# A hybrid decoder layer on one core: gate matmuls dealt one at a time, three score banks a head for one query block, and five small reorderings

## The chip, the cores and the metric

The kernel runs on one core of a Trainium2 chip. The core has a matmul engine (TensorE, PE in the rows below), a vector engine (DVE), a scalar engine (ACT), a general-purpose engine (GpSimd, POOL) and a queue engine that issues most transfers (SyncE, SP). Matmul results land in PSUM, of which the kernel uses eight banks of 128x512 float32. The metric is the device time of one execution in microseconds (us).

## The reference

One decoder layer on 1024 tokens of width 1024, all in float32:

```python
h   = rmsnorm(x, norm_mix)
(q, kc, vc, ks, vs, kw, vw, nsa_g, rq, rk, rv, rg, gate_a, gate_b) = split(h @ w_in)
A   = nsa(q, ...)        # 8 heads: compressed + selected + sliding-window attention, gated per head
B   = retention(rq, rk, rv) * silu(rg)      # 4 heads, chunks of 128, decaying state
x   = x + (sigmoid(gate_a) * (A @ w_proj_a) + sigmoid(gate_b) * (B @ w_proj_b)) @ w_out
x   = x + square(relu(rmsnorm(x, norm_mlp) @ w_up)) @ w_down
y   = rmsnorm(x, norm_final)
```

With 1024 tokens there are 16 blocks to select and 16 are selected, so the selected branch is plain causal attention. Window: 512 keys. Compressed keys: one for every 16 tokens.

## The kernel before

Every float32 matmul is made of three: an operand X is split into a rounded part (`h`, written by an ACT copy) and the rest (`l`, a DVE subtraction), and h·h, h·l and l·h are summed in one PSUM bank. The order of PE is written out by hand for the whole program; in two stretches (the first 60 us and the one called border) the other engines' order is written out too. Elsewhere a scheduler orders ACT, DVE, POOL and SP around PE's fixed order. Within an engine everything is first in, first out.

The stages, by the time of the profiled execution:

- **Start and retention (0 to 240 us).** Weights arrive in 128x1024 pieces in a ring of three buffers named `raw` (pool `wraw`) and are split into `wh` and `wl`. Token tiles are normed, transposed (`tp`) and split into `bh`, `bl`. For the first two tiles the norm factor is applied late: `ret_v` scales, `renorm_sum` (POOL, into its own buffer `yr`) and `renorm` rebuild the tile. `ret_v` makes the values `v` (ACT, then DVE) and the swish gate: `th`, a tanh on ACT, and `y` on DVE. For each chunk PE transposes queries and keys, computes `pS`, `pO` and the state `pD`, whose operand `t` is the low half of the keys (L352 on DVE).
- **Keys, values and queries (240 to 362 us).**
- **Attention and gates (362 to 760 us).** Eight query blocks, 7 down to 0, times two key groups times two pairs of heads make 32 units. A unit has `scores` (matmuls into banks named `S`, masks and a running minimum on DVE at L1008, exponentials on ACT at L1017 into `pS`, the selected, and `pW`, window and compressed, and a scaling on POOL at L1029), then, one unit later, `pv` (transposes into banks `pt` at L1064 and L1065, split by ACT at L1066 and DVE at L1067 into `ph`, `pl`, and matmuls into bank `O`). `prep_q` transposes a group's queries (L952) and splits them into `QQ` and `ql`. In between come the matmuls of the two merge gates: 32 gates of 24 matmuls of 128x512 into a bank named `gps`, each closed by a tanh on ACT (`gst`, L920). PSUM is dealt as four `S` banks, two `pt` banks, one `gps` and one `O`. From gate 15 on, odd gates use an `S` bank.
- **Projections, output and the border (760 to 960 us).** `bh`, `bl` are overwritten by the mix. In the border, eight tiles are multiplied by the second half of `w_out` (`mmu`), added to the residual (`add_x`: `x1t`, L1378), transposed two tiles later (L1342), scaled (`y`, L1346), and combined into the forms that a Strassen-like product of the next stage needs: `first_tile` for tiles 0 to 3, `second_tile` for tiles 4 to 7. `high` is the ACT copy, `lows` the DVE subtraction that follows (L1337).
- **The two MLP products (960 to 1550 us)** and the last norm.

What sets the order in the attention stage is a list of events with fractional places: each generator (`scores`, `pv`, `prep_q`, the gates) is cut at its `yield`s, `place(it, n, lo, hi)` spreads `n` pieces evenly over an interval, and PE's program is the sorted list. `GATES` says how many pieces of the gates fall in each unit's interval. A gate yields after every third matmul.

Of the kernel before, what the change touches and what calls it, by code (L numbers as in the profile page):

```python
# [9 lines left out]
F32 = mybir.dt.float32  # L10
# [7 lines left out]
P = 128  # L18
S = 1024
# [90 lines left out]
def hybrid_block(ctx: ExitStack, tc: tile.TileContext, a: dict, out: bass.AP):  # L110
# [44 lines left out]
    def mm(o, w, m, start, stop):  # L155
        T.matmul(o, w, m, start=start, stop=stop)  # L156
# [62 lines left out]
    with ExitStack() as es:  # L219
# [12 lines left out]
        with ExitStack() as e1:  # L232
# [54 lines left out]

            def renorm_sum(j, q):
                js, ks = slice(j * P, (j + 1) * P), slice(4 * q, 4 * q + 4)
                y = tpb.tile([P, 4, P], F32, name="yr", bufs=1)  # L290
                G.tensor_tensor(y, bh[:, ks, js].bitcast(F32), bl[:, ks, js].bitcast(F32), op=OP.add)
                return y

# [88 lines left out]

            def ret_v(j, c, ps):
                raw = c == 0 and j < RAW
                if raw:
                    v = tmp.tile([P, 2, 2, P], F32R, name="v", tag="v")
                    src = ps[:, :256].rearrange("p (n d) -> p n d", n=2)
                    A.activation(v[:, :, 0], src, AF.Copy, scale=rs_raw[j])
                    V.scalar_tensor_tensor(v[:, :, 1], src, rs_raw[j], v[:, :, 0], op0=OP.mult, op1=OP.subtract)
                else:  # L390
                    v = hl(ps[:, :256], "v", 2)
                th = tmp.tile([P, 256], F32, name="th", tag="th")
                A.activation(th, ps[:, 256:], AF.Tanh, scale=hrs_raw[j] if raw else 0.5)
                y = tmp.tile([P, 256], F32, name="y")
                V.scalar_tensor_tensor(y, th, 1.0, ps[:, 256:], op0=OP.add, op1=OP.mult)
                return v, y
# [44 lines left out]
            with tc.manual_schedule(engines={eng.PE, eng.Pool, eng.DVE, eng.Activation, eng.SP}):  # L441
# [20 lines left out]
                def w_hi(w):  # L462
                    A.activation(w[1], w[0], AF.Copy)
# [33 lines left out]
                lo = [split_half(y0[q], 0, q) for q in range(2)]  # L497
                warm_up(2)
                banks = [bank(j) for j in range(3)]
                w_hi(ws[1])  # L500
                w_lo(ws[0])
                ws.append(w_dma(3))
                xs.append(load_norm(3))
# [398 lines left out]
    def gate_pieces(n):  # L902
        pool = gpool["p"]
        i, th = divmod(n, 2)
        dst, ii = (ga_scr, i) if i < 8 else (gb_scr, i - 8)
        ts = slice(th * 512, (th + 1) * 512)
        gate_w(i)
        gate_w(i + 1)
        h, l = gw[i]
        if n % 2 and n >= GALT and gpool["alt"] is not None:  # L910
            ps = gpool["alt"].tile([P, 512], F32, name="gps", tag="S")
        else:
            ps = pool.tile([P, 512], F32, name="gps", bufs=1)
        parts = [(h, k, x) for k in range(KD) for x in (bh, bl)] + [(l, k, bh) for k in range(KD)]
        for m, (w, k, x) in enumerate(parts):
            mm(ps, w[:, k * P:(k + 1) * P], x[:, k, ts], m == 0, m == len(parts) - 1)
            if m % 3 == 2 and m < len(parts) - 1:
                yield
        o = gsp.tile([P, 512], F32, name="gst")
        A.activation(o, ps, AF.Tanh, scale=0.5)  # L920
        nc.sync.dma_start(dst[ii, :, th], o)
        yield
# [13 lines left out]
    with ExitStack() as e3:  # L936
# [10 lines left out]
        gpool["p"], gpool["alt"] = psO, psS  # L947

        def prep_q(qb, g):
            tp = psT.tile([P, 4, P], F32, name="pt", tag="pt")  # L950
            for h in range(4):
                T.transpose(tp[:, h], qs[qb, g][:, h], ident)  # L952
            QQ = at.tile([P, 4, P], F32R, name="QQ")
# [5 lines left out]
            if nxt < 16:  # L959
                load_q(7 - nxt // 2, nxt % 2)  # L960
            yield

        def scores(qb, g, hp, u):
            QQ, ql = qs[qb, g]
# [10 lines left out]
            for i in range(2):  # L975
# [4 lines left out]
                pS = at.tile([P, 1024], F32, name="pS", bufs=PS_S)  # L980
                pW = at.tile([P, 768], F32, name="pW", bufs=PS_S)
                G.memset(pW[:, 704:], 0.0)
                for base, KK, start, width, p in ((1, KKs, 0, cS, pS), (2, KKw, w0, cW, pW)):
                    groups = []
                    for c0 in range(0, width, 512):
                        n = min(512, width - c0)
                        groups.append([(base if c0 == 0 else base + 2, KK, start + c0, n,
                                        mask(c0, n, width, base == 2), p[:, c0:c0 + n])])
                    split = len(groups) > 1
                    if base == 2:  # L990
                        tail = (0, KKc, 0, 64, cmp_m[:, 56 - 8 * qb:120 - 8 * qb], pW[:, 640:704])
                        if groups[-1][0][3] <= 448:
                            groups[-1].append(tail)
                        else:
                            groups.append([tail])
                    exps = []
                    for gi, grp in enumerate(groups):
                        ps = psS.tile([P, 512], F32, name="S")
                        off = 0
                        done = []  # L1000
                        for b, K, c0, n, mk, o in grp:
                            done.append((b, ps[:, off:off + n], mk, o))
                            off += n
                        _, K, c0 = grp[0][:3]
                        mm(ps[:, :off], QQ[:, h], K[:, g, c0:c0 + off], True, False)
                        mm(ps[:, :off], ql[:, h], K[:, g, c0:c0 + off], False, True)
                        for b, sc, mk, o in done:
                            V.tensor_tensor_reduce(sc, sc, mk, -0.125, BIGPOS, OP.add, OP.min, mx[:, b:b + 1])  # L1008
                            exps.append((b, sc, o))
                        if gi < len(groups) - 1:  # L1010
                            yield
                    if split:
                        V.tensor_tensor(mx[:, base:base + 1], mx[:, base:base + 1], mx[:, base + 2:base + 3],
                                        op=OP.min)
                    for b, sc, o in exps:
                        m = b - 2 if b > 2 else b
                        A.activation(o, sc, AF.Exp, bias=mx[:, m:m + 1], scale=-1.0, accum_out=sums[:, b:b + 1])  # L1017
                    if base == 1:
# [66 lines left out]

        def n_scores(qb):
            sel, win = (qb + 4) // 4, (min(qb + 1, 5) + 3) // 4 + (1 if qb == 3 else 0)
            return 2 * (sel + win)

        def n_pv(qb):  # L1090
            return 2 * ((qb + 1 + min(qb + 1, 5) + 2) // 2)
# [22 lines left out]
            place(it, n_pv(qb) - 1, n, n + 1 + V_END)  # L1114
            place(it, 1, n + 1 + V_LAST, n + 1 + V_LAST)
        for n, k in enumerate(GATES):
            place(gate_it, k, n - 1, n)
        next(prep_q(7, 0))
        for ev in sorted(todo, key=lambda v: v[:2]):
            if len(ev) > 3:  # L1120
# [121 lines left out]
    with ExitStack() as e5:  # L1242
# [80 lines left out]
        with ExitStack() as e6:  # L1323
# [25 lines left out]
            def first_tile(j):  # L1349
                js = cols(j)  # L1350
                high("11", raw_t[j, 0], bh[:, :4, js], bl[:, :4, js])
                high("21", raw_t[j, 1], bh[:, 4:, js], bl[:, 4:, js])
                lows("11", "21")
                V.tensor_sub(raw_t[j, 0], raw_t[j + 4, 0], raw_t[j, 0])

# [345 lines left out]
```

## Time and profile before

| | |
|---|---|
| Median of 3 runs (lowest, highest) | 1564.6 us (1562.92, 1568.26) |
| Profiled execution, its own time | 1563.77 us |
| Profiled execution, span of its instructions | 1562.0 us |
| Mean granted PE clock | 0.999 |
| Busy share of the span: PE, DVE, ACT, POOL | 99%, 69%, 47%, 27% |
| PE matmuls | 7845 |

A row of the waits view says which engine and line waited, for whom, the total in us, how often, and the longest. A row of the timeline has the start, the duration, engine, line, operation, output<-input, shape and, in brackets, how long the engine sat idle before it and who released it. Matmuls overlap: a 128x512 matmul has a duration of 0.39 us, but in a stream of them one starts every 0.22 to 0.23 us, so PE's busy share hides waits of less than about 0.16 us and shows the rest too short.

### The profile page before, as it was taken

The numbers are of one execution on the slowest core, as the hardware profiler recorded it, in microseconds if no ns is written. First come the engines' busy times: TensorE is split into PE (matmuls) and PEld (weight loads), VectorE is DVE, ScalarE is ACT, GpSimd is POOL, SyncE is SP. The second block draws the span as 40 slices with busy tenths as digits, with TensorE's granted clock in tenths as the row PEclk, the third lists the DMA queues.
The fourth block names the chain that finished last, engine by engine and source line by source line (L and its number), as shares of the span: only waits on it lengthen the run. The fifth ranks groups of instructions, "written<-read, shape, count | busy, mean of one in ns | idle before, by whom it ended". The sixth has DMA issues, their size and how long they took to land.

```text
span 1562.0 us, 22775 instructions
## 1 busy us (share of the span) xinstructions
PE 1542.2 (99%) x7845; PEld 1293.8 (83%) x7845; DVE 1080.8 (69%) x2237; ACT 730.9 (47%) x1657; POOL 423.6 (27%) x516
## 2 busy tenths in 40 slices
PE   9999999999999999999999999999999999999997
PEld 7788888988888888888888888888888888888886
DVE  6875663765777777776765379877777667876673
ACT  6663553764677776766522234222222244443452
POOL 3120010002333333333000001744455446521320
PEclk9999999999999999999999999999999999999999
DMA  6202111342111112121644332544444597764472
GB/s 227 68 18 65 58 32 26 112 152 78 48 35 55 48 35 61 43 68 55 198 147 153 109 112 91 188 149 152 158 156 148 185 381 242 219 210 124 148 271 87
DMA packets 98900, 191.85 MB, mean 123 GB/s; under 512 B 26632, under 2 KB 30096, under 8 KB 98784
## 3 DMA queue, kind: packets, MB, share of 16 engines
q1 hardware_dynamic: 97008, 185.82, 36.2%
q0 software_dynamic: 944, 2.93, 0.5%
q10 hardware_dynamic: 832, 1.64, 0.3%
q8 instruction: 62, 1.02, 0.3%
q14 instruction: 54, 0.44, 0.1%
HBM read 140.02 MB, written 50.33 MB: 122 GB/s over the span
## 4 chain that ended last, share of the span: by engine, by line
PE 86%; DVE 6%; ACT 3%; issue 2%; POOL 0%; DMA 0%; POOLq 0%; ACTq 0%; DVEq 0%
PE mmu L156 23%; PE mm L156 20%; PE mmd L156 19%; PE gps L156 9%; PE S L156 4%; PE O L156 4%; PE pt L1065 2%; PE pt L1064 2%; ACT pW L1017 1%; PE pO L156 1%; DVE pl L1067 1%; PE pc L156 1%; DVE S L1008 1%; ACT pS L1017 0%; ACT ph L1066 0%
## 5 line engine op out<-in xcount | busy, mean ns | idle before, releaser
L1217 DVE TENSOR_TENSOR wl<-raw,wh 128x1024 fp32r<-128x1024 f32 x121 | 183.7, 1543 | 67.3 <-ACT wh L1216 66.0
L1216 ACT ACTIVATE wh<-raw 128x1024 fp32r<-128x1024 f32 x121 | 125.1, 1056 | 205.4 <-PE mmd L156 127.7
L156 PE MATMUL mmd<-wh 128*128 128x512 f32 x448 | 174.3, 389 | 0.0
L156 PE MATMUL mmd<-wl,wh 128*128 128x512 f32 x448 | 174.3, 389 | 0.0
L156 PE MATMUL mmd<-wh,wl 128*128 128x512 f32 x448 | 174.3, 389 | 0.0
L156 PE MATMUL mm<-wh,bh 128*128 128x512 f32 (+1 forms) x416 | 160.9, 390 | 1.6 <-ACT bh L271 1.0
L156 PE MATMUL mm<-wh,bl 128*128 128x512 f32 (+1 forms) x416 | 155.0, 376 | 0.0
L156 PE MATMUL mm<-wl,bh 128*128 128x512 f32 (+1 forms) x416 | 154.3, 375 | 0.0
L1067 DVE TENSOR_TENSOR pl<-pt,ph 128x512 fp32r<-128x512 f32 (+1 forms) x160 | 103.8, 649 | 35.9 <-ACT ph L1066 33.4
L1066 ACT ACTIVATE ph<-pt 128x512 fp32r<-128x512 f32 (+1 forms) x160 | 90.3, 568 | 55.2 <-PE pt L1065 54.3
L1029 POOL TENSOR_SCALAR pS<-pS,cf 128x512 f32<-128x512 f32 (+7 forms) x80 | 54.6, 688 | 225.7 <-ACT ph L1066 73.8
L1008 DVE CUSTOM_DVE_ANT_0 S<-S,edge_m 128x512 f32<-128x512 f32 (+3 forms) x192 | 100.8, 530 | 13.8 <-PE S L156 11.2
L156 PE MATMUL gps<-bl,wh 128*128 128x512 f32 x256 | 104.1, 407 | 0.0
L156 PE MATMUL gps<-bh,wh 128*128 128x512 f32 x256 | 103.1, 403 | 0.5 <-ACT gst L920 0.5
L1298 POOL TENSOR_TENSOR sf<-raw 128x512 f32<-128x512 f32 x14 | 22.9, 1633 | 294.2 <-DVE wl L1217 294.2
L156 PE MATMUL mmu<-bh,wh 128*128 128x512 f32 x256 | 99.7, 389 | 0.0
L156 PE MATMUL mmu<-bh,wl 128*128 128x512 f32 x256 | 99.6, 389 | 0.0
L156 PE MATMUL mmu<-bl,wh 128*128 128x512 f32 x256 | 99.6, 389 | 0.0
L156 PEld LDWEIGHTS mmd<-wh,wl 128*128 128x128 f32 x448 | 84.1, 188 | 17.6
L156 PEld LDWEIGHTS mmd<-wh 128*128 128x128 f32 x448 | 84.1, 188 | 17.5
L156 PEld LDWEIGHTS mmd<-wl,wh 128*128 128x128 f32 x448 | 84.1, 188 | 17.3
L156 PEld LDWEIGHTS mm<-wh,bl 128*128 128x128 f32 x416 | 78.1, 188 | 15.4 <-DVE bl L286 0.4
(362 smaller groups left out, 4033.9 us busy)
## 6 DMA issues: line engine op xcount, KB each, us to landing
raw<-u_scr SPq DMA_DIRECT2D x56, 512.0 KB, 3.9
raw<-w_down SPq DMA_DIRECT2D x41, 512.0 KB, 4.8
raw<-w_up SPq DMA_DIRECT2D x32, 512.0 KB, 3.6
u_scr<-u SPq DMA_DIRECT2D x59, 256.0 KB, 2.2
u_scr<-s SPq DMA_DIRECT2D x42, 256.0 KB, 2.0
y<-w_down SPq DMA_DIRECT2D x14, 512.0 KB, 8.3
x<-x SPq DMA_DIRECT2D x8, 512.0 KB, 5.6
qt<-q_scr SPq DMA_DIRECT2D x32, 128.0 KB, 2.4
```

Of the source, the lines that this page charges most:

```text
L156: T.matmul(o, w, m, start=start, stop=stop)
L1008: V.tensor_tensor_reduce(sc, sc, mk, -0.125, BIGPOS, OP.add, OP.min, mx[:, b:b + 1])
L1017: A.activation(o, sc, AF.Exp, bias=mx[:, m:m + 1], scale=-1.0, accum_out=sums[:, b:b + 1])
L1029: G.tensor_scalar(v, v, cf[:, b:b + 1], 1.0, op0=OP.mult, op1=OP.mult)
L1064: T.transpose(tp[:, bi * 2], p0, ident)
L1065: T.transpose(tp[:, bi * 2 + 1], p1, ident)
L1066: A.activation(ph[:, :n], tp[:, :n], AF.Copy)
L1067: V.tensor_sub(pl[:, :n], tp[:, :n], ph[:, :n])
L1216: A.activation(h[:, :n], r, AF.Copy)
L1217: V.tensor_sub(l[:, :n], r, h[:, :n])
L1298: eng.tensor_tensor(F[:, 1], x11, x21, op=OP.subtract)
```

## The change

Seven edits, in the order of the program:

1. The renormed sums (POOL) go to a `raw` buffer of the weight ring, not to `yr`. The loads of the weights `w_r1a`, which share that ring, come later in SP's order.
2. In `ret_v`, for the first two tiles, the tanh is recorded ahead of the DVE instruction that makes the low half of `v`.
3. The second piece of the first weights is copied by ACT in two halves.
4. A gate yields after every matmul; three times as many pieces are placed over the same intervals.
5. `prep_q` transposes into an `S` bank (tile `qT`), not into a `pt` bank.
6. For query block 4 a head's scores use three `S` banks and not four: selected 0 to 511; selected rest, window rest and compressed together; window 0 to 511. The instructions are the same in number and shape, but for the order.
7. In the border, the low halves of `first_tile` are made in a step of their own, `first_lows`, behind the next tile's `add_x`.

```diff
             def renorm_sum(j, q):
                 js, ks = slice(j * P, (j + 1) * P), slice(4 * q, 4 * q + 4)
-                y = tpb.tile([P, 4, P], F32, name="yr", bufs=1)
+                y = wraw.tile([P, 1024], F32, name="raw", tag="raw")[:, :512].rearrange("p (k t) -> p k t", k=4)
...
             def ret_v(j, c, ps):
                 raw = c == 0 and j < RAW
+                th = tmp.tile([P, 256], F32, name="th", tag="th")
                 if raw:
                     v = tmp.tile([P, 2, 2, P], F32R, name="v", tag="v")
                     src = ps[:, :256].rearrange("p (n d) -> p n d", n=2)
                     A.activation(v[:, :, 0], src, AF.Copy, scale=rs_raw[j])
+                    A.activation(th, ps[:, 256:], AF.Tanh, scale=hrs_raw[j])
                     V.scalar_tensor_tensor(v[:, :, 1], src, rs_raw[j], v[:, :, 0], op0=OP.mult, op1=OP.subtract)
                 else:
                     v = hl(ps[:, :256], "v", 2)
-                th = tmp.tile([P, 256], F32, name="th", tag="th")
-                A.activation(th, ps[:, 256:], AF.Tanh, scale=hrs_raw[j] if raw else 0.5)
+                    A.activation(th, ps[:, 256:], AF.Tanh, scale=0.5)
...
                 banks = [bank(j) for j in range(3)]
-                w_hi(ws[1])
+                for c in (slice(0, 512), slice(512, 1024)):
+                    A.activation(ws[1][1][:, c], ws[1][0][:, c], AF.Copy)
                 w_lo(ws[0])
...
             mm(ps, w[:, k * P:(k + 1) * P], x[:, k, ts], m == 0, m == len(parts) - 1)
-            if m % 3 == 2 and m < len(parts) - 1:
+            if m < len(parts) - 1:
                 yield
...
         def prep_q(qb, g):
-            tp = psT.tile([P, 4, P], F32, name="pt", tag="pt")
+            tp = psS.tile([P, 4, P], F32, name="qT", tag="S")
...
+        def packed(qb):
+            return qb == 4
...
+                tail = (0, KKc, 0, 64, cmp_m[:, 56 - 8 * qb:120 - 8 * qb], pW[:, 640:704])
+                if packed(qb):
+                    groups = [parts[1][:1], parts[1][1:] + parts[2][1:] + [tail], parts[2][:1]]
+                    ready = [(), (1, 0), (2,)]
+                else:
+                    groups = [[v] for v in parts[1] + parts[2]]
...
+                    for K, c0, o0, n in runs:
+                        mm(ps[:, o0:o0 + n], QQ[:, h], K[:, g, c0:c0 + n], True, False)
+                        mm(ps[:, o0:o0 + n], ql[:, h], K[:, g, c0:c0 + n], False, True)
...
         def n_scores(qb):
             sel, win = (qb + 4) // 4, (min(qb + 1, 5) + 3) // 4 + (1 if qb == 3 else 0)
-            return 2 * (sel + win)
+            return 2 * (3 if packed(qb) else sel + win)
...
         for n, k in enumerate(GATES):
-            place(gate_it, k, n - 1, n)
+            place(gate_it, 3 * k, n - 1, n)
...
                 high("11", raw_t[j, 0], bh[:, :4, js], bl[:, :4, js])
                 high("21", raw_t[j, 1], bh[:, 4:, js], bl[:, 4:, js])
+
+            def first_lows(j):
                 lows("11", "21")
                 V.tensor_sub(raw_t[j, 0], raw_t[j + 4, 0], raw_t[j, 0])
...
                     add_x(j, 1, x1t, ps)
-                    if n and n % 2 == 0:
+                    if n % 2:
+                        first_lows(j - 4)
+                    elif n:
                         lows("2", "3", "1", "4", "22")
```

Three places show how instructions move. Each list is an engine's program order, with no time in it.

**PE where one gate ends and the next begins**, in the unit of query block 7 whose heads come second (the end of gate 3; a gate's last eight matmuls read `wl`, its first reads `bh` and `wh`). Before:

```order
L156 MATMUL gps<-bh,wl 128x512 x3
L156 MATMUL O<-pl,Vw 64x256
L156 MATMUL O<-ph,Vw 128x256
L156 MATMUL O<-pl,Vw 64x256
L156 MATMUL O<-ph,Vw 128x256
L1064 MATMUL pt<-ident,pS 128x128
L1065 MATMUL pt<-ident,pS 128x128
L1064 MATMUL pt<-ident,pS 128x128
L1065 MATMUL pt<-ident,pS 128x128
L156 MATMUL O<-pl,Vw 64x256
L156 MATMUL O<-ph,Vw 128x256
L156 MATMUL O<-pl,Vc 64x256
```

One more matmul into `O` follows there, and then the next gate's first three. With the change:

```order
L156 MATMUL gps<-bh,wl 128x512 x2
L156 MATMUL O<-pl,Vw 64x256
L156 MATMUL O<-ph,Vw 128x256
L156 MATMUL O<-pl,Vw 64x256
L156 MATMUL O<-ph,Vw 128x256
L156 MATMUL gps<-bh,wh 128x512
L1075 MATMUL pt<-ident,pS 128x128
L1076 MATMUL pt<-ident,pS 128x128
L1075 MATMUL pt<-ident,pS 128x128
L1076 MATMUL pt<-ident,pS 128x128
```

Between the two gates, which write the same bank, stood four transposes and eight matmuls into `O`; now four matmuls into `O` stand there. It is so at twelve ends of gates, of query blocks 7, 6 and 5. At the end of gate 1 nothing stands between any more (before, two matmuls of 128x512 did, as in the rows at 370.93 us that the prediction shows for gate 0); gates 14 and later have other banks or a longer way.

**DVE at the end of the border**, tile 3's scaling up to tile 7's residual sum and what follows. Before:

```order
L1346 TENSOR_TENSOR y_10935<-tp,gcol 128x512
L1337 TENSOR_TENSOR bl<-y_10436,bh 128x4x128
L1337 TENSOR_TENSOR bl<-y_10935,bh 128x4x128
L1354 TENSOR_TENSOR y_10436<-y_10610,y_10436 128x512
L1378 TENSOR_TENSOR x1t<-mmu,x1t 128x512
L1217 TENSOR_TENSOR wl<-raw,wh 128x1024
```

With the change:

```order
L1357 TENSOR_TENSOR y_10928<-tp,gcol 128x512
L1391 TENSOR_TENSOR x1t<-mmu,x1t 128x512
L1348 TENSOR_TENSOR bl<-y_10429,bh 128x4x128
L1348 TENSOR_TENSOR bl<-y_10928,bh 128x4x128
L1367 TENSOR_TENSOR y_10429<-y_10603,y_10429 128x512
L1228 TENSOR_TENSOR wl<-raw,wh 128x1024
```

The sum `x1t` of tile 7 has moved ahead of the two low halves of tile 3.

**ACT at the first chunk of retention** (v, t: values and keys; `sml`: scores). Before:

```order
L388 ACTIVATE v<-mm,fac 128x2x128
L351 ACTIVATE t_831<-qk 128x2x128
L362 ACTIVATE sml<-pS 128x256
L393 ACT_TABLE_LOAD
L393 ACTIVATE th<-mm,fac 128x256
L351 ACTIVATE s<-sm 128x2x128
L351 ACTIVATE t_928<-qk 128x2x128
```

With the change:

```order
L389 ACTIVATE v<-mm,fac 128x2x128
L390 ACT_TABLE_LOAD
L390 ACTIVATE th<-mm,fac 128x256
L362 ACTIVATE sml<-pS 128x256
L351 ACTIVATE t_832<-qk 128x2x128
L351 ACTIVATE s<-sm 128x2x128
L351 ACTIVATE t_929<-qk 128x2x128
```

The table load and the tanh stand before the score copy; in the same stretch an ACT copy and a DVE subtraction of `w_r1a` (128x1024 each) have left for a place some 35 us later.

More of the change, by code (lines that the diff above doesn't have):

```diff
@@ L982, in scores @@
                 G.memset(pW[:, 704:], 0.0)
+                parts = {}
                 for base, KK, start, width, p in ((1, KKs, 0, cS, pS), (2, KKw, w0, cW, pW)):
[L984 to L993, printed above, removed]
-                        else:
[L995 to L1018, printed above, removed]
+                    parts[base] = [(base if c0 == 0 else base + 2, KK, start + c0, min(512, width - c0),
+                                    mask(c0, min(512, width - c0), width, base == 2), p[:, c0:min(width, c0 + 512)])
+                                   for c0 in range(0, width, 512)]
@@ new lines, in scores @@
+                tail = (0, KKc, 0, 64, cmp_m[:, 56 - 8 * qb:120 - 8 * qb], pW[:, 640:704])
[4 more added lines that the diff above has]
+                    groups = [[v] for v in parts[1] + parts[2]]
+                    if groups[-1][0][3] <= 448:
+                        groups[-1].append(tail)
+                    else:
+                        groups.append([tail])
+                    ready = [()] * len(groups)
+                    ready[len(parts[1]) - 1] = (1,)
+                    ready[-1] = (2, 0)
@@ new lines, in scores @@
+                exps = {0: [], 1: [], 2: []}
+                for grp, rdy in zip(groups, ready):
+                    ps = psS.tile([P, 512], F32, name="S")
+                    off, runs, done = 0, [], []
+                    for b, K, c0, n, mk, o in grp:
+                        done.append((b, ps[:, off:off + n], mk, o))
+                        if K is KKc and runs:
+                            runs[-1][3] += n
+                        else:
+                            runs.append([K, c0, off, n])
+                        off += n
+                    for K, c0, o0, n in runs:
+                        mm(ps[:, o0:o0 + n], QQ[:, h], K[:, g, c0:c0 + n], True, False)
+                        mm(ps[:, o0:o0 + n], ql[:, h], K[:, g, c0:c0 + n], False, True)
+                    for b, sc, mk, o in done:
+                        V.tensor_tensor_reduce(sc, sc, mk, -0.125, BIGPOS, OP.add, OP.min, mx[:, b:b + 1])
+                        exps[b - 2 if b > 2 else b].append((b, sc, o))
+                    for m in rdy:
+                        if len(exps[m]) > 1:
+                            V.tensor_tensor(mx[:, m:m + 1], mx[:, m:m + 1], mx[:, m + 2:m + 3], op=OP.min)
+                    for m in rdy:
+                        for b, sc, o in sorted(exps[m], key=lambda v: v[0]):
+                            A.activation(o, sc, AF.Exp, bias=mx[:, m:m + 1], scale=-1.0, accum_out=sums[:, b:b + 1])
+                    if grp is not groups[-1]:
```

## The prediction

> **What bounds the kernel now.** I read the page's first part and the windows by stage first: which engine is full, and where not. Core 0; the columns are the time, then busy us and (x) instructions of PE, its weight loads, DVE, ACT and POOL, then the PE clock, the DMA share and GB/s.
>
> ```profile
> 362.00:500.00 138.00, 135.54 (x830) 115.54 (x829) 102.90 (x357) 94.31 (x268) 44.04 (x75) 1.00 0.16 49
> 500.00:640.00 140.00, 138.44 (x878) 119.47 (x877) 107.98 (x366) 98.89 (x284) 46.76 (x91) 1.00 0.16 48
> 640.00:760.00 120.00, 117.86 (x706) 101.17 (x705) 81.76 (x294) 80.41 (x243) 37.12 (x102) 1.00 0.23 70
> 960.00:1540.00 580.00, 580.00 (x2560) 480.42 (x2559) 422.78 (x422) 191.08 (x221) 253.65 (x157) 1.00 0.56 189
> ```
>
> PE sets the time everywhere, at clock 1.00: in the last row it never stands, and the change touches nothing in that stage. In the attention stage (362 to 760 us) it stands 2.46 + 1.56 + 2.14 = 6.2 us. DVE is busy three quarters of it, so only orders and buffers can make PE wait. No edit changes how many matmuls there are; the change can move only PE's waits. So the second view is the waits of PE (total us, times, longest):
>
> ```profile
> PE pt L1065 <- POOL pS L1029: 1.7, 4, 1.0
> PE S L156 <- ACT pS L1017: 1.3, 2, 0.9
> PE O L156 <- DVE pl L1067: 0.8, 2, 0.4
> PE pD L156 <- DVE t L352: 0.8, 1, 0.8
> PE pt L952 <- DVE pl L1067: 0.7, 1, 0.7
> PE S L156 <- DVE ql L956: 0.6, 2, 0.4
> PE mm L156 <- ACT wh L463: 0.5, 1, 0.5
> PE gps L156 <- ACT gst L920: 0.5, 2, 0.2
> PE tp L1342 <- DVE x1t L1378: 0.5, 1, 0.5
> PE S L156 <- ACT QQ L955: 0.4, 1, 0.4
> ```
>
> These ten rows come to 7.8 us, half a per cent of 1562.0: all that the change aims at. What one wait costs is read from a timeline, here at the end of gate 0 (start, duration, engine, output<-input, shape; in brackets the idle time and its releaser):
>
> ```profile
> 370.25 0.85 PE L156 MATMUL gps<-bh,wl 128*128 128x512 f32 x3
> 370.93 0.39 PE L156 MATMUL S<-KKw,QQ 128*128 128x512 f32 x1
> 371.16 0.39 PE L156 MATMUL S<-KKw,ql 128*128 128x512 f32 x1
> 371.78 0.50 PE L156 MATMUL gps<-bh,wh 128*128 128x512 f32 x1 [0.23 <-ACT gst L920]
> 372.12 0.40 PE L156 MATMUL gps<-bl,wh 128*128 128x512 f32 x1
> 372.35 0.39 PE L156 MATMUL gps<-bh,wh 128*128 128x512 f32 x1
> ```
>
> and on ACT:
>
> ```profile
> 371.13 0.60 ACT L920 ACTIVATE gst<-gps 128x512 f32<-128x512 f32 x1 [0.81 <-PE gps L156]
> ```
>
> In a stream one 128x512 matmul starts 0.23 us after the other (370.93 to 371.16). After a wait the next but one starts 0.34 later (371.78 to 372.12) and then 0.23 again: a wait costs its idle time and 0.11 for refilling. The same rows give the **turn of a gate**. Its last matmul starts 0.23 before 370.93, at 370.70; the tanh starts at 371.13, 0.43 later, and takes 0.60; the next gate's first matmul starts 0.05 after it. In all 1.08 us during which PE needs other work.
>
> **The change part by part.** I sum against the profiled execution's own time, 1563.8; the median of the runs is 1564.6, so 0.8 is added at the end.
>
> *First weights in two halves.* PE waits 0.5 for this copy:
>
> ```profile
> 9.62 1.06 ACT L463 ACTIVATE wh<-raw 128x1024 fp32r<-128x1024 f32 x1 [1.02 <-DMA raw<-w_r0a]
> ```
>
> A 128x512 copy takes about 0.60 on ACT, as the tanh of that shape does, so the first half is there 0.4 earlier. **−0.4** (0 to −0.6; nothing if a later piece of the same weights is then late).
>
> *Tanh and sums.* The wait of 0.8 for `t` goes back over DVE to ACT:
>
> ```profile
> 67.14 0.41 ACT L351 ACTIVATE t<-qk 128x256 fp32r<-128x256 f32 x1
> 67.85 1.28 ACT L393 ACT_TABLE_LOAD   x1
> 69.14 0.47 ACT L393 ACTIVATE th<-mm,fac 128x256 f32<-128x256 f32 x1
> ```
>
> and on DVE:
>
> ```profile
> 69.65 0.42 DVE L395 SCALAR_TENSOR_TENSOR y<-th,mm 128x256 f32<-128x256 f32 x1 [0.77 <-ACT th L393]
> 71.33 0.75 DVE L352 TENSOR_TENSOR t<-qk,t 128x256 fp32r<-128x256 f32 x2
> ```
>
> With the change the table load stands ahead of the copy of 67.14, 0.7 earlier; DVE, which sat idle 0.77 for `th`, runs that much sooner, and the last DVE row follows in its queue. ACT's copies of `t` and the scores now come behind the load, but DVE reads them only behind `y`: the last row of DVE is 2.2 us behind the load's end (69.13). **−0.7** (0 to −0.9). A 128x1024 pair of copy and subtraction leaves this place for one some 35 us later, where nothing waits for it yet: nothing added. The Trainium skill, "ScalarE: Activation LUTs", has a figure for a table switch, but the row of 1.28 us is used.
>
> *The queries' transposes in an S bank.* The wait of 0.7 (L952, for the `pt` bank that `pl` empties) loses its cause. The rival bank is free if the heads before have been read; at a group's start they have, as `QQ` of the last group is then done with. **−0.8** with the refill (0.3 to −0.8).
>
> *Three banks a head in block 4.* The wait for the exponential `pS` is one for a bank:
>
> ```profile
> 574.78 0.40 PE L156 MATMUL S<-KKw,ql 128*128 128x512 f32 x1
> 576.06 0.36 PE L156 MATMUL S<-KKw,QQ 128*128 128x192 f32 x1 [0.89 <-ACT pS L1017]
> ```
>
> Two of these, 1.3 us, both in block 4. The bank asked for is given back by the exponential of four banks before; a head of three banks asks for one less, and the same matmuls lie between. **−1.5** (0 to −1.5).
>
> *Gates dealt one at a time, gains.* Three matmuls of a gate between pieces of a unit become one, at three times as many places, so gaps between a transpose and what DVE or POOL make of it become more even. I counted the PE work between writer and reader: it grows by about 0.46 us ahead of the `O` matmuls that wait for `pl`, and at three of the four waits for POOL's `pS`. The 0.8 (two waits) go: **−1.0**. Of the 1.7, one wait of 1.0 stays, as its distance is the same:
>
> ```profile
> 674.52 0.33 PE L1065 MATMUL pt<-ident,pS 128*128 128x128 f32 x1 [1.02 <-POOL pS L1029]
> ```
>
> The other three go: **−1.0**. Both lie between 0 and that.
>
> *The same edit, losses.* The order lists show twelve ends of gates where four matmuls into `O` now lie between the last matmul of one gate and the first of the next, which write one bank; before, four transposes and eight such matmuls did.
>
> ```profile
> 392.64 0.28 PE L156 MATMUL O<-ph,Vw 128*128 128x256 f32 x1
> 392.75 0.28 PE L156 MATMUL O<-pl,Vw 128*64 128x256 f32 x1
> ```
>
> One of these starts 0.11 to 0.12 after the other. Before: 0.23 + 12 × 0.12 = 1.6 us of cover for 1.08, no wait. Now: 0.23 + 4 × 0.12 = 0.71; PE waits 1.08 − 0.71 = 0.37, with the refill 0.48. Twelve times: **+5.8**. The least is 0, were ACT to take the tanh before its bank's last matmul, which cannot be; the least that the rows allow is 12 × 0.37 = 4.4. What stands behind the waiting matmul is all of PE's queue. While PE stands, DVE and POOL go on, so this wait also pays for a part of others, which is why I give no further loss to them.
>
> The tanh starts 0.43 after the matmul only if ACT is free. Where it has a copy to make first it is later:
>
> ```profile
> 439.32 0.85 PE L156 MATMUL gps<-bh,wl 128*128 128x512 f32 x3
> ```
>
> ```profile
> 440.32 0.60 ACT L1066 ACTIVATE ph<-pt 128x512 fp32r<-128x512 f32 x1
> 440.80 0.61 ACT L920 ACTIVATE gst<-gps 128x512 f32<-128x512 f32 x1
> ```
>
> The last of these three matmuls starts 0.39 before 440.17, at 439.78, and the tanh 1.02 after it, 0.59 too late. Four gates of the twelve stand so in the trace of before, which would be 2.4 more; but the transposes that feed `ph` now come behind the turn, so I take less than half: **+1.0** (0 to 2.4). At the end of gate 1 two 128x512 matmuls, 0.46, leave the gap, **+0.4**. The copies `QQ` and `ql` have 0.23 less PE work before their readers at two places, **+0.5** (0 to 0.5).
>
> *Border.* PE's first matmuls of the next product, tile 7's residual sum, and DVE:
>
> ```profile
> 942.55 0.39 PE L156 MATMUL mmu<-wh,bl 128*128 128x512 f32 x1
> 943.00 0.39 PE L156 MATMUL mmu<-bl,wh 128*128 128x512 f32 x1
> 944.76 0.66 PE L1342 MATMUL tp<-ident,x1t 128*128 128x128 f32 x4 [0.46 <-DVE x1t L1378]
> ```
>
> ```profile
> 942.03 1.47 DVE L1337 TENSOR_TENSOR bl<-y,bh 128x512 fp32r<-128x512 f32 x2
> 944.02 0.68 DVE L1378 TENSOR_TENSOR x1t<-mmu,x1t 128x512 f32<-128x512 f32 x1
> ```
>
> The sum `x1t` of tile 7 now stands ahead of tile 3's low halves. It needs the matmul that ends at 942.94, so it runs from about 943.0 to 943.6, and the first low half from there to 944.3. But PE's matmul of 943.00 reads that low half: it starts 1.33 later, 1.44 with the refill, while the wait of 0.46 at 944.76 and its refill of 0.16 go. **+0.8** (−0.6 if PE reads other columns of `bl` first, to +1.5).
>
> The sum: −0.4 − 0.7 − 0.8 − 1.5 − 1.0 − 1.0 = −5.4; 5.8 + 1.0 + 0.4 + 0.5 + 0.8 = +8.5; together +3.1, so 1566.9 for a profiled execution and 1564.6 + 3.1 = 1567.7 for the median. I say **1567.5**.
>
> **The rivals.** *The finer deal clears the stage.* The same pauses at the turns let DVE, ACT and POOL get ahead, and all other standing of the attention stage goes: the 6.2 us of the windows and 17 refills of 0.11, −8.1, beside −1.1 ahead of the stage, against 5.8 + 0.4 + 0.8 for the turns and the border: −2.2, 1562.4. For it: waits of 0.2 or 0.4 us are most of the rows. Against it: the longest one (674.52) keeps its distance.
>
> *The tanh stands behind copies at every turn* (the slower side). If ACT's queue has a `ph`, an exponential or a `wh` ahead of `gst`, as at 440.80, every turn is 0.59 worse: 12 × 0.59 = 7.1 in place of my 1.0, 1573.8. It decides wherever `gst` starts later than 0.43 after its last matmul. For it: ACT is two thirds busy (94.31 of 138). Against: at 371.13 it was idle 0.81 before.
>
> *The packing moves nothing.* From gate 15 on an odd gate holds one of four S banks; if that is the one missing in block 4, three banks a head wait as four did, and the queries' transposes take one more: the −1.5 fall away, 1569.2. For it: the wait is on a bank. Against it: two heads of three banks each leave more matmuls between any two uses.
>
> *The clock falls.* Twelve short pauses might throttle PE. The row at 674.52 is a pause of 1.02 us inside a window of clock 1.00, and no row shows a pause that cost clock. The Trainium skill says in "TensorE: Matmul & The Clock Gate", section "A second HAM failure mode: psum-queue depth-cycling", that a kernel which cycles through PSUM banks can idle often enough between groups for the clock to swing between half and full. By that page's window of 3.4 us, half a window's work lost at each turn would be an estimate of 12 × 1.7 = 20 us. The trace's clock of 1.00 over thirteen waits speaks against it.
>
> **How the numbers follow.** A difference of less than 0.3%, 4.7 us, can't be told from no change, so "faster" begins below 1559.9 and "slower" above 1569.3. Main forecast 0.46, its own range 1564 to 1570; clearing 0.28; tanh behind copies 0.16; packing 0.08; clock 0.02. Clearing is faster by over 0.3% only where the border's price falls away too and ACT keeps up at the turns, 0.11 of its 0.28; the main case adds 0.01: faster 0.12. Slower: 0.15 of the tanh case, 0.02 of the clock, 0.03 of the packing and 0.07 of the main case: 0.27. The rest, 0.61, is no change. The range reaches from below clearing's 1562.4 to just short of the tanh case's 1573.8: 1561 to 1573.
>
> **What would show it.** The waits of PE should have a row of `gps` for `gst` with ten or more waits and 4 to 7 us in place of 0.5; no row of L952; the row of `S` for `pS` gone or under 0.4; the row of `t` under 0.3; a wait of `mmu` for `bl` of 1 us or more near 944 in place of that of `tp`. In timelines `gst` should start 0.43 after its last matmul, where ACT is free. The prediction is wrong if the turns show no wait (the scheduler has put other work there), if `gst` comes a whole instruction later at most turns, or if the stages after 960 us change their length.

## The result: 0.56% slower, and the profile after

The changed kernel takes 1572.8 us (median of 4 runs, 1572.67 to 1573.42); the kernel before, beside it, 1563.8 (4 runs, 1562.92 to 1568.26). The ratio is 1.0056, 95% interval 1.0043 to 1.0069. It is slower by some 9 us; the forecast was 3 us slower, 1567.5 in a range of 1561 to 1573. The direction was right and the range just held, but more than half of the loss was not foreseen.

The span of the profiled execution went from 1562.0 to 1571.6 us. To see where, I cut it at PE's own instructions. These rows are the gates' matmuls, in the kernel before (the last two numbers are the first and the last start):

```profile
L156 PE MATMUL gps<-bh,wh x256: 387/395/499, 362.3 to 759.2; 128*128 128x512 f32 x128
L156 PE MATMUL gps<-bh,wl x256: 387/393/485, 368.2 to 761.2; 128*128 128x512 f32 x128
```

and in the changed kernel:

```profile
L156 PE MATMUL gps<-bh,wh x256: 387/396/507, 363.4 to 768.0; 128*128 128x512 f32 x128
L156 PE MATMUL gps<-bh,wl x256: 386/395/487, 369.5 to 770.0; 128*128 128x512 f32 x128
```

| stretch, us | before | after | difference | forecast |
|---|---|---|---|---|
| start to first gate matmul | 362.3 | 363.4 | +1.1 | −1.1 |
| first to last gate matmul ("the gates' stretch") | 398.9 | 406.6 | +7.7 | +3.4 |
| first to last matmul `mmu`, with the border | 399.9 | 400.7 | +0.8 | +0.8 |
| the other pieces (87.3, 304.6 and 9.0) | | | 0.0 | 0 |

The 7845 matmuls are the same in number and shape, so these are waits. The waits of PE in the changed kernel:

```profile
PE gps L156 <- ACT gst L922: 2.7, 9, 0.7
PE O L156 <- DVE pl L1078: 2.4, 7, 0.5
...
PE mmu L156 <- DVE bl L1348: 1.2, 1, 1.2
PE pt L1076 <- POOL pS L1040: 1.1, 2, 0.9
PE S L156 <- DVE ql L958: 0.8, 2, 0.4
PE S L156 <- ACT QQ L957: 0.8, 1, 0.8
PE pD L156 <- DVE t L352: 0.6, 1, 0.6
...
PE pO L156 <- DVE v L352: 0.4, 1, 0.4
PE S L156 <- ACT pS L1028: 0.4, 1, 0.4
```

The gates now wait nine times for their tanh, as forecast, but the view adds this up to 2.7 us where 4 to 7 were expected. The wait of the queries' transposes (L952 before) is gone, and so are the two of `S` for `pS` in block 4; the 0.4 that is left is a new one at 511 us. The two waits of `O` for `pl` that were to vanish have vanished, but seven others came, at places that had none. There is a new wait of `pO` in the retention stage, and `QQ` and `ql` are late as forecast.

One turn of a gate, the end of gate 2, PE and then ACT:

```profile
395.32 0.27 PE L156 MATMUL O<-ph,Vw 128*128 128x256 f32 x1
395.82 0.50 PE L156 MATMUL gps<-bh,wh 128*128 128x512 f32 x1 [0.22 <-ACT gst L922]
396.15 0.27 PE L1075 MATMUL pt<-ident,pS 128*128 128x128 f32 x1
```

```profile
395.17 0.60 ACT L922 ACTIVATE gst<-gps 128x512 f32<-128x512 f32 x1 [0.34 <-PE gps L156]
```

The first matmul of the next gate would have started at 395.32 + 0.12 = 395.44 and starts at 395.82, 0.38 later, and what follows it comes 0.33 later and not 0.23. So this turn costs 0.38 + 0.10 = 0.48, the forecast's number. The bracket shows 0.22 of it.

The border, PE and then DVE:

```profile
951.66 0.39 PE L156 MATMUL mmu<-bh,wh 128*128 128x512 f32 x1
953.21 0.50 PE L156 MATMUL mmu<-bl,wh 128*128 128x512 f32 x1 [1.16 <-DVE bl L1348]
```

```profile
951.86 0.69 DVE L1391 TENSOR_TENSOR x1t<-mmu,x1t 128x512 f32<-128x512 f32 x1 [1.39 <-PE mmu L156]
952.47 1.28 DVE L1348 TENSOR_TENSOR bl<-y,bh 128x512 fp32r<-128x512 f32 x2
```

It went as worked out: the sum of tile 7 takes DVE from 951.86, the low halves come behind it, and PE's second matmul of the next product starts 953.21 − 951.66 = 1.55 after the first and not 0.23.

### The profile page after: what moved, and what is told of

Its sections match the earlier page's. It is cut to its first block, busy times and chain, and to the rows that moved or that the text cites. A ratio compares the mean times of both kernels' runs of the same rounds, so it can differ in the third digit from the quotient of the medians.

```text
span 1571.6 us, 22746 instructions
## 1 busy us (share of the span) xinstructions
PE 1549.1 (99%) x7845; PEld 1292.3 (82%) x7845; DVE 1085.1 (69%) x2237; ACT 729.2 (46%) x1658; POOL 421.6 (27%) x516
## 4 chain that ended last, share of the span: by engine, by line
PE 82%; DVE 8%; ACT 5%; issue 2%; POOL 1%; DMA 0%; POOLq 0%; ACTq 0%; DVEq 0%
PE mmu L156 25%; PE mmd L156 19%; PE mm L156 18%; PE gps L156 8%; PE S L156 3%; PE O L156 3%; DVE pl L1078 2%; PE pt L1076 2%; PE pt L1075 1%; ACT pW L1028 1%; DVE S L1021 1%; ACT ph L1077 1%; PE pc L156 1%; ACT pS L1028 1%; PE pO L156 1%
```

## The experiments

The theory was that the dealing by single matmuls makes the loss in the gates' stretch; the rivals were that the S banks do (queries' transposes and packed heads take them), and, for the waits of `O`, that ACT's queue does. The runs below are single executions, except e9, and the stretches are read from their traces: the pieces behind the gates that no edit touches repeat within 0.05 us (but for the tail of e8, 0.9 longer), and the gates' stretch within 0.5: 406.6 in the changed kernel, 406.8 in e4 and 407.1 in e6, whose order of matmuls in that stretch is the same. The time up to the first gate matmul differs by as much as a microsecond between executions whose code there is the same (a wait for `bh` at 8 us alone is 0.3 to 1.9 us), so small gains ahead of it can be told only in shorter stretches, between the same two matmuls.

### e1 and e2: the dealing alone, and all but the dealing

e1 is the kernel before with this edit alone, e2 the changed kernel with it undone:

```diff
-            if m % 3 == 2 and m < len(parts) - 1:
+            if m < len(parts) - 1:
                 yield
...
-            place(gate_it, k, n - 1, n)
+            place(gate_it, 3 * k, n - 1, n)
```

> The kernel before with one edit, the gates dealt by single matmuls. The stretch from the first to the last matmul of a gate took 398.9 us before and 406.6 in the changed kernel. Theory (the dealing makes the whole loss): the stretch is longer than the 406.6 of the changed kernel, 408 to 410, since the gains of the packing and of the queries' bank are missing, and the execution is 9 to 11 us longer than before; gates wait for their tanh at six turns or more. Rival (the S banks: the queries' transposes and the packed heads take banks that the scores want): the stretch is 400 to 402.

> The changed kernel with the gates dealt by three again, all other edits kept. Theory (dealing): the stretch of the gates falls from 406.6 to 396 to 397.5, below the 398.9 of before, and no wait of a gate for its tanh is longer than 0.3 us. Rival (S banks): it stays above 404.

Measured: e1 1575.4 us, stretch 411.0, that is +12.1 by this one edit. e2 1563.7 us, stretch 397.8. The dealing costs 8.8 us beside the other edits (406.6 − 397.8). It is the whole loss of the stage; the S banks are not. e1 was worse than expected since the queries' transposes, still in a `pt` bank, now wait there four times, 4.0 us:

```profile
PE pt L952 <- DVE pl L1067: 4.0, 4, 1.4
PE gps L156 <- ACT gst L920: 3.0, 11, 0.7
```

e2's stretch is 1.0 below before where 2.3 was promised, so the two bank edits fell short too. It also waits six times for `pl` (2.2 us), four of them in block 4 like those of the changed kernel from 563 us on, so these four are not the dealing's.

### e3 and e7: the bank edits

e3 is the kernel before with both bank edits; e7 has only the queries' transposes:

```diff
         def prep_q(qb, g):
-            tp = psT.tile([P, 4, P], F32, name="pt", tag="pt")
+            tp = psS.tile([P, 4, P], F32, name="qT", tag="S")
```

> The kernel before with two edits: the queries' transposes in an S bank and three banks a head in block 4. Theory (dealing): these two give what the prediction said, 0.8 + 1.5 = 2.3 us: the stretch of the gates is 396 to 397.5 and the two waits of S for the exponentials in block 4 are gone. Rival (S banks): the stretch is 402 or more, with waits of S or of the transposes for DVE or ACT.

> The kernel before with one edit: the queries' transposes in an S bank. The prediction gave it 0.8 us. Theory (a cause removed): the stretch of the gates is 398.0 or less in place of 398.9, and the waits of O for pl stay at two. Rival (pl is late for whoever comes next): the wait of L952 for pl goes, 0.7, and O waits for pl five times or more in its place, so that the stretch is 398.6 to 399.5.

Measured: e7's stretch is 397.4, −1.5, twice the forecast, and the waits of `O` stay at two. e3's is 398.2, and e2's, whose matmuls are in the same order, was 397.8. So packing on top of the queries' bank costs 0.5 to 0.8, where it was to give 1.5. Its waits of `S` are gone in e3, and four of `O` for `pl` came in block 4. At the end of gate 13, e7's ACT makes a `ph` ahead of the window's exponentials:

```profile
551.82 0.60 ACT L1066 ACTIVATE ph<-pt 128x512 fp32r<-128x512 f32 x1 [0.45 <-PE pt L1065]
552.38 0.69 ACT L1017 ACTIVATE pW<-S,mx 128x512 f32<-128x512 f32 x1
```

e3 at the same place, ACT and PE:

```profile
552.10 0.69 ACT L1026 ACTIVATE pS<-S,mx 128x512 f32<-128x512 f32 x1 [2.02 <-DVE mx L1023]
...
554.32 0.22 ACT L1026 ACTIVATION_READ_ACCUMULATOR pW<-S,mx 128x1 f32 x1
554.42 0.61 ACT L1075 ACTIVATE ph<-pt 128x512 fp32r<-128x512 f32 x1
```

```profile
555.87 0.33 PE L156 MATMUL O<-pl,Vw 128*64 128x256 f32 x1 [0.40 <-DVE pl L1076]
```

With three banks a head the exponentials of `pS` need the packed second bank as well, and ACT sits idle 2.02 us for it; then all the exponentials come in one row of ten instructions, and the `ph` that was made at 551.82 stands behind them, at 554.42. `pl` and `O` are late after it.

### e4 and e5: the turn of the gate one place later

Both were to issue a gate's first matmul one place later, so that more of the other work stands between two gates.

```diff
         for m, (w, k, x) in enumerate(parts):
+            if m == 0:
+                yield
             mm(ps, w[:, k * P:(k + 1) * P], x[:, k, ts], m == 0, m == len(parts) - 1)
-            if m < len(parts) - 1:
+            if 0 < m < len(parts) - 1:
                 yield
```

> The changed kernel, but the first matmul of a gate is issued with its second, one place later, so that twice as much other work lies between the last matmul of a gate and the first of the next. Theory that the turn of the one bank is the price (last matmul to tanh 0.43, tanh 0.60, next matmul 0.05): the waits of the gates for their tanh, 2.7 us in nine, fall under 0.8, and the stretch from 406.6 to 402 or 403. Rival (ACT's queue: its copies stand ahead of the ph that pl needs, whatever the place of the gate): the 2.4 us in seven waits of O for pl stay or grow as the pause at the turns goes, and the stretch stays above 404.5.

e4 had `m == 1` in the added line, which moves the `yield` from behind matmul 0 to ahead of matmul 1: the same order. It was in effect a second execution of the changed kernel, 1573.7 us with a stretch of 406.8, and tells only how well one repeats. e5 is the edit as shown.

> The changed kernel with the first matmul of each gate truly one place later (its own place is left empty, the next holds two), so that between gates 2 to 17 stand eight to twelve matmuls of O and mostly four transposes, 1.37 us or more of cover as with the dealing by three, and not 0.70. Theory turn: the waits of gates for the tanh go (2.7 us in nine becomes 0.5 in two, as before), with their refills 3.5 to 4 us; the stretch of the gates falls from 406.6 to 402.5 to 403.5. Theory ACT's queue: the waits of O for pl grow from 2.4 us by 1.5 or more, since the pause at the turn was covering them, and the stretch stays above 404.5. If the dealing by single matmuls costs nothing else, the stretch comes down to 398, the value of all edits but the dealing.

Measured: 1567.6 us, stretch 401.6. The turns cost 5.0 us (406.6 − 401.6); the gates' waits are back at two.

```profile
PE O L156 <- DVE pl L1080: 3.2, 8, 0.7
...
PE gps L156 <- ACT gst L924: 0.5, 2, 0.2
```

The stretch fell even further than either theory said. The waits of `O` grew by 0.8, so a little had been covered by the pauses, and 3.7 of the 8.8 are still there (401.56 − 397.84): not the turns.

### e6: the sums

```diff
             def renorm_sum(j, q):
-                y = wraw.tile([P, 1024], F32, name="raw", tag="raw")[:, :512].rearrange("p (k t) -> p k t", k=4)
+                y = tpb.tile([P, 4, P], F32, name="yr", bufs=1)
```

> The changed kernel with the renormed sums in their own buffer again (one of the ring's buffers before). Theory (the sums in the ring move DVE's and POOL's order): the waits of pO for v at 103 and 112 us, 0.13 and 0.53 in the changed kernel, go, and the first gate matmul comes 0.6 to 0.9 earlier. Rival (the tanh ahead of v's low half makes them, since that DVE instruction is recorded later): they stay. The wait of pD for t, 0.6 now, stays at 0.6 if the tanh alone cut it from 0.8, and goes to 0.3 or less if the sums' order had eaten the tanh's gain.

Measured: the waits of `pO` are gone, and that of `t` stays at 0.6. So the sums in the ring caused the waits of `pO`. The first gate matmul comes at 362.3, 1.1 earlier than in the changed kernel, but only half of that is the edit. Between the same two matmuls, those that start at 60.06 and 120.02 us in the kernel before, the traces take:

| kernels | from 60 to 120 us |
|---|---|
| neither edit: before, e1, e3, e7 | 59.93 to 60.02 |
| early tanh, sums in `yr`: e6, e9, e10, e11 | 60.11 to 60.15 |
| early tanh, sums in the ring: the changed kernel, e2, e4, e5, e8 | 60.61 to 60.67 |

The sums cost 0.5, and the early tanh by itself costs a little where it was to gain 0.7. From there to the first gate matmul the changed kernel takes 243.0 us, and e2, e4, e5 and e8, with the same code there, 242.1 to 242.5: the rest of the 1.1 is chance. What the sums do is seen on DVE in the changed kernel, and on PE:

```profile
105.39 1.23 DVE L214 TENSOR_TENSOR wl<-raw,wh 128x1024 fp32r<-128x1024 f32 x1 [0.17 <-ACT wh L213]
...
110.02 0.61 DVE L427 SCALAR_TENSOR_TENSOR z<-o,rh,y 128x128 f32<-128x128 f32 x2 [1.14 <-POOL rh L425]
...
111.49 0.42 DVE L352 TENSOR_TENSOR v<-mm,v 128x256 fp32r<-128x256 f32 x1
```

```profile
111.96 0.45 PE L156 MATMUL pO<-v,s 128*128 128x256 f32 x2 [0.42 <-DVE v L352]
```

The first row is the subtraction of `w_r1a` that left its old place at 72 us with the edit. It now stands ahead of the chain that leads from `o` over ACT and POOL to `rh`, so `rh` comes late; DVE waits for it, and `v` stands behind `z` in DVE's queue. In the kernel before that same instruction `z` started at 108.22, and `v` was done 1.5 us ahead of its reader. The edit removed one buffer and reordered ACT, DVE and SP.

### e8: the weights' copies taken from ACT

```diff
-            A.activation(h[:, cs], r[:, cs], AF.Copy)
+            G.tensor_copy(h[:, cs], r[:, cs])
```

for the gates' weights only.

> The changed kernel with the copies that make wh of the gates' weights taken from ACT to POOL (64 copies of 128x512; ACT has some 0.55 each, 35 us of its queue). Theory ACT's queue: with no wh ahead of ph and of the tanh, the tanh starts 0.43 after its gate's last matmul at nearly every turn and the waits of O for pl fall from 2.4 us under 1.0. Rival (DVE, three quarters busy, makes pl late by itself): the waits of O for pl stay over 2. POOL has the copies ahead of its scaling of pS, so waits of the transposes for POOL may grow, whichever theory is right; the total time is no test here.

Measured: stretch 404.3. The tanh starts 0.42 to 0.44 after its gate's last matmul at all of gates 0 to 13, as that theory said; the waits of `O` for `pl` stay at 2.4 us, in six, which it did not. The weights' copies are not what makes `pl` late.

### e9: the parts that pay, and one number

```diff
-GALT = 15
+GALT = 19
```

on top of the kernel before with the queries' transposes in an S bank, the first weights in two halves and the early tanh. `GALT` is the gate from which odd gates use an S bank.

> The kernel before with the three edits that the stretches show as gains or as free (queries' transposes in an S bank, weights in two halves, tanh ahead of v's low half; the sums in their old buffer) and one number: odd gates use an S bank from gate 19 on, not from gate 15, so that no gate holds one of the four S banks while query block 4 takes four a head. Theory (gate 15 held the bank for which block 4 waited): the two waits of S for the exponentials in block 4, 1.3 us and 1.65 with refills, go without packing, no wait of O for pl comes in their place, and the stretch of the gates is 395.5 to 396 in place of 397.4 with the queries' bank alone. Rival (four banks a head are too few by themselves): the waits stay and the stretch is 397 or more. The tanh ahead and the halves: the first gate matmul 0.3 to 0.7 earlier than before if each gives what the prediction said, 0.3 or less if the wait of pD for t stays near 0.6. In all 1559.5 to 1561.5 beside 1563.8, ratio 0.997 to 0.999.

Measured: 1560.7 us (median of 11 runs, 1559.73 to 1561.46) against 1563.7 (15 runs), ratio 0.998, interval 0.9971 to 0.9989; it beats both kernels. The gates' stretch is 395.65. In the attention stage only these waits are left:

```profile
PE pt L1067 <- POOL pS L1031: 1.5, 3, 1.0
PE O L156 <- DVE pl L1069: 0.8, 2, 0.4
PE S L156 <- DVE ql L958: 0.6, 2, 0.4
PE gps L156 <- ACT gst L922: 0.5, 2, 0.3
PE S L156 <- ACT QQ L957: 0.4, 1, 0.4
```

The waits of `S` in block 4 went without packing, with no wait of `O` in their place. Gate 15, which held one of the four S banks at that time, had been their cause. The wait for `t` stays at 0.6, as in the changed kernel. The first gate matmul came 0.6 earlier than before, but e1, which has none of these early edits, came as early. The halves' worth shows in a shorter stretch: between the two matmuls that start at 9.02 and 13.13 us in the kernel before, the four kernels without the halves take 3.87 to 4.10 and the nine with them 3.58 to 3.75, some 0.3 less.

### e10 and e11: what the dealing costs besides the turns

e10 is e9's kernel with the gates dealt by single matmuls (the edit of e1) and the turn of e5. e11 is e10 with `S_BEG` and `S_END` 0.07 of a unit larger, which puts the scores later.

> The kernel of the run before this one (queries' bank, halves, tanh, odd gates in an S bank from gate 19 on; stretch of the gates 395.65 us) with the gates dealt by single matmuls, each gate's first matmul one place later, so that the turns are covered and no packing or missing bank is in the way. Theory (single matmuls cost by themselves, since with two and not three matmuls of a gate between two pieces of a unit some transposes come later against the scores, and ACT makes their ph behind the next six instructions of the exponentials): the five waits of O for pl in the odd places of query blocks 6 and 5 (440 to 501 us; 2.7 us with refills in the run with the turn one later) stay, the stretch is 398.5 to 400. Rival (the price beside the turn was the packing's): waits of O for pl as in the run before, two, and a stretch of 395.5 to 396.5.

> The kernel of the run before this one, with the scores' pieces 0.07 of a unit later (about 1 us), so that the transposes stand earlier against them. In the run before, O waited for pl at the ends of gates 5, 6, 7, 8 and 9 (440, 456, 471, 486, 501 us); there ACT has two ph behind the three exponentials of the unit's window and compressed scores, where the kernel that deals by three has one (and at gates 5 and 7 two with one more ahead). With the scores later, ACT's order has one ph behind the exponentials at gates 6, 8 and 9 and still two at gates 5 and 7. Theory (ph behind the exponentials makes pl late): the waits at gates 6, 8 and 9 go, those at 5 and 7 stay. Rival (the distance of two gate matmuls between transposes and O is too short by itself): all five stay. The total is no test, as waits for the scores themselves may come.

Measured: e10 1563.5 us, stretch 398.4, just under the theory's 398.5: with turns covered and no packing, single matmuls cost 2.7 (398.4 − 395.65). `O` waits at the five places named. To see why, here is ACT in the kernel before ahead of the end of gate 5:

```profile
436.34 1.08 ACT L1066 ACTIVATE ph<-pt 128x512 fp32r<-128x512 f32 x2
437.97 0.69 ACT L1017 ACTIVATE pW<-S,mx 128x512 f32<-128x512 f32 x1 [0.54 <-DVE mx L1013]
```

and the same place in the changed kernel, ACT, DVE and PE:

```profile
438.52 0.59 ACT L1077 ACTIVATE ph<-pt 128x512 fp32r<-128x512 f32 x1
439.00 0.64 ACT L185 ACTIVATE wh<-raw 128x512 fp32r<-128x512 f32 x1
440.00 0.69 ACT L1028 ACTIVATE pW<-S,mx 128x512 f32<-128x512 f32 x1 [0.36 <-DVE mx L1025]
...
441.21 0.20 ACT L1028 ACTIVATION_READ_ACCUMULATOR pW<-S,mx 128x1 f32 x1
441.30 0.60 ACT L1077 ACTIVATE ph<-pt 128x512 fp32r<-128x512 f32 x1
```

```profile
441.94 0.69 DVE L1078 TENSOR_TENSOR pl<-pt,ph 128x512 fp32r<-128x512 f32 x1
```

```profile
442.69 0.33 PE L156 MATMUL O<-pl,Vw 128*64 128x256 f32 x1 [0.29 <-DVE pl L1078]
```

Before, two `ph` are made ahead of the six exponential instructions; now one is, and the other waits behind them from 440.00 to 441.30. Its `pl` follows at 441.94, and `O` at 442.69. In the two traces the transposes that this `ph` copies start 0.66 us (before) and 1.16 us (after) after the head's last pair of score matmuls began (435.43 and 436.09, 437.41 and 438.57): with the even dealing they stand half a microsecond later, and the scheduler put the exponentials ahead.

e11 tests this. Its order on ACT has one `ph` fewer behind the exponentials at the ends of gates 6, 8 and 9, and not at 5 and 7. Measured: the waits at gates 6, 8 and 9 are gone, and those at 5 and 7 stand (at 440.54 and 471.11 us, 0.30 and 0.53). So at these gates the order of `ph` and exponentials decides. It doesn't make a wait everywhere: at gates 2 to 4 of e10 two `ph` stand behind the exponentials as well, and `O` doesn't wait there. As a kernel e11 is worse, 1570.9 us: with the scores later, `pS` comes late from POOL.

```profile
PE pt L1069 <- POOL pS L1033: 8.7, 11, 1.8
...
PE O L156 <- DVE pl L1071: 0.8, 2, 0.5
```

## Why the prediction was right or wrong

The direction held, and the range held by 0.2 us, but that is partly luck. The range had been drawn to just short of a rival with another cause, the main forecast's own range ended at 1570, and "slower" had been given 0.27 beside 0.61 for no change. Inside the sum, the turns (7.2 forecast, 5.0 measured) and the queries' transposes came out better, and the gains of the finer dealing, the packing, and tanh and sums came out worse, each of these with the wrong sign.

- **Where the loss lies** (right). PE's waits carry all of it, the stage after the border is unchanged to 0.05 us, and the clock stayed at 0.999 with all these pauses. The Trainium skill, "TensorE: Matmul & The Clock Gate", section "A second HAM failure mode: psum-queue depth-cycling", tells of a kernel whose clock swings because PE idles briefly between groups of matmuls; this case's trace does not show it.
- **Turn of a gate** (right mechanism and price, total too high). Forecast 5.8 + 1.0, and 0.4 for gate 1, measured 5.0 (e5). The plain turn costs the 0.48 that was worked out. Not all twelve pay it in full: at gates 5 to 9 the matmuls of `O` inside the turn wait for `pl` first and use part or all of the time.
- **Tanh behind copies** (rival, wrong cause though nearest in time). 1573.8 was worked out for it and 1572.8 measured, but in the changed kernel the tanh starts 0.42 to 0.45 after the last matmul at all turns up to gate 12 but two (gates 5 and 7, 0.78 and 0.76), and late at gate 13 (1.39). The forecast's own small share for it was nearer the mark.
- **Gains of the finer dealing** (wrong, the largest error). The step that failed is "it grows by about 0.46 us ahead of the `O` matmuls that wait for `pl`". That was counted only at places that already waited. Those two waits are gone, as forecast. But at places that had slack, the ends of gates 5 to 9, the transposes moved later against the scores, ACT's order flipped, and five new waits of `O` came, two of them under 0.1 in the changed kernel; the four others there, in block 4, are the packing's (e2 and e3 have them). Apart from the turns the dealing costs 2.7 us (e10), where −2.0 for the gains and +0.5 for `QQ` and `ql` had been entered. Of the three waits for POOL that were to go, two went and one stayed at 0.26. Some 1.0 of the 8.8 appears only beside the packing and was not taken apart; half of that is within what the stretch differs between executions.
- **Packing** (wrong). "−1.5" was +0.5 to +0.8. The bank wait went as forecast, but the exponentials come in one late row on ACT, with `ph`, `pl` and `O` behind it, the same flip of ACT's order as with the dealing. The rival "the packing moves nothing" had the true cause of the wait, the S bank held by gate 15 (e9), though not the outcome.
- **Queries' transposes** (right, too small). −0.8 forecast, −1.5 measured (e7). The price of a wait was taken as idle time and 0.11; but the idle time in a bracket counts from the end of the last matmul, 0.39 after its start, and a stream would have started the next 0.23 after it. So each wait costs 0.16 more than that. This wait's bracket said 0.73; from the matmul ahead of it (391.02) to the one behind it (392.44) are 1.42 us, and 0.47 in e7, so it cost 0.95. The rest holds a wait for POOL at 747.7 (0.21) that e7 doesn't have and e3, with the same edit, has again, so a part of the −1.5 may be chance.
- **Tanh and sums** (wrong). −0.7 forecast, +0.7 measured from 60 to 120 us (e6). Two steps failed. One is "DVE, which sat idle 0.77 for `th`, runs that much sooner": the wait for `t` fell only from 0.75 to 0.58. The tanh is early as forecast, but DVE's low half of `v`, here before and after, now stands behind it:

```profile
67.33 0.47 DVE L389 SCALAR_TENSOR_TENSOR v<-mm,fac,v 128x256 fp32r<-128x256 f32 x1
```

```profile
68.82 0.48 DVE L391 SCALAR_TENSOR_TENSOR v<-mm,fac,v 128x256 fp32r<-128x256 f32 x1 [1.07 <-ACT th L390]
```

DVE used to make that half while it waited; now it sits idle 1.07 and does it after. The other is the pair of `w_r1a` that leaves for a place "where nothing waits for it yet: nothing added". At its new place its subtraction, 1.23 us on DVE, makes `v` late for `pO`, and undoing the edit that moved it gains 0.5 (e6).
- **First weights in two halves** (right). −0.4 forecast, some −0.3 measured (e9).
- **The clearing rival** counts 17 refills, which is the number of waits in all ten rows; 14 of them lie in the attention stage, and its 1562.4 should have been 1562.8.
- **Border** (right). +0.8 forecast, +0.8 measured, in every kernel with that edit and in none without it.

## What to carry to other kernels

When work on a full engine is spread more evenly, look at every place where a bank or a buffer changes hands, and at the order that the other engines' queues take from it; a count at the places that wait today says nothing about those with slack. Read what a wait costs from the starts of the matmuls around it, not from the idle time in the bracket, which is too low. Where a buffer is scarce, ask who holds it before making the user smaller: one number freed the bank, while packing made new waits.

## What the runs showed of the hardware

The hand-over of a bank from PE to ACT and back is constant to 0.01 us where both are free: 0.43 from the start of the last 128x512 matmul to the tanh, 0.60 for the tanh, 0.05 to the next matmul. Nine waits of PE that the view adds up to 2.7 us, 2.2 more than before, went back to two with the edit of e5, which gained 5.0 us. The brackets leave out 0.16 of each wait and the 0.10 to 0.11 that the matmul behind it starts late; for seven waits that makes 2.2 + 7 × 0.27 = 4.1, and the rest was not taken apart.
